# Attention turns in written groups: one TensorE order from the q columns to the output projection

## The chip, the cores and the metric

One core of a Trainium2 chip runs the kernel. The metric is device time in microseconds (us), the median of several runs; a profiled run, taken by itself, gives the trace. The engines are TensorE (PE, with its weight loads as PEld), VectorE (DVE), ScalarE (ACT), GpSimd (POOL) and SyncE (SP, which issues most DMAs).

## The reference, cut to what matters

The model is two layers over 256 tokens of width 2048, in float32. Layer one is an RWKV mixer, which this change leaves alone. Layer two is an attention with three branches that share keys and values by group; the change lies in it.

```python
proj = u @ w_in                                   # 16 heads of q, 48 gate columns, z
q = rope_partial(proj[..., :2048].reshape(B, T, 16, 128), arange(T))
gates = sigmoid(proj[..., 2048:2096] + gate_b)
# per head, with the keys of its group (4 heads to a group):
o_cmp = softmax(q @ k_cmp.T * scale, visible) @ v_cmp      # 15 compressed blocks
o_sel = softmax(q @ k_sel.T * scale, causal) @ v_sel       # all 4 blocks are selected
o_win = softmax(q @ k_win.T * scale, causal) @ v_win       # window 512 > 256 tokens
o = gates[0] * o_cmp + gates[1] * o_sel + gates[2] * o_win
h = h + (o * silu(z)) @ w_o
```

## The kernel before, in words

All large products are done in float32 precision as three products of a high and a low part (`whi`, `wlo` of a weight, `mx` or `ob` pairs of an activation): high by high, high by low, low by high. The weights come as raw pieces by SP's DMAs; for each unit ACT copies the high part (L213) and DVE subtracts to get the low one (L192; every third unit of the attention stage goes to POOL). Units are split three ahead of their use.

The stages are: normalisation and the columns of the RWKV mixer, its scan, its output projection with the residual, the kv columns with the compression (`phase_kv`), the attention stage, and the last output projection (`phase_bo`).

The attention stage has 21 dense phases, in the order of QZ (L81): five blocks of q columns (`phase_q`, 432, 512 and three times 384 columns, 16 k steps of six matmuls) and sixteen z columns (`phase_z`, heads 15 down to 0, each 16 k steps of a 512- and a 256-column matmul). The attention of the heads, pairs of heads from 7 down to 0, goes on beside them in background tasks. `Sched` (L97) holds a counter `sch.t`: each dense step yields its estimated nanoseconds, and after each the background tasks whose time has come go one step further. So the counter decides where in the program an instruction stands. Before, the program's place is only a rank for the scheduler of the framework, which orders each engine's queue by readiness in its own timeline and by rank; attention instructions on TensorE rank 1,000 places ahead (`atPE` in PRI, L93). The hardware then runs each engine's queue in order.

For one pair of heads the work is:

- q: a block is copied out of PSUM with its row scale (L1775), rotated on DVE (`rope`, L1628 to L1633), and turned on TensorE (transposed, two 128 x 128 pieces to a head, L1789) into a PT bank; ACT copies the high part, DVE subtracts the low one (L1792, L1793).
- scores (`weigh`, per head): nine matmuls (three parts, over 800 columns in all) into `pair0`, the only score tile, two PSUM banks wide; DVE adds masks and takes maxima (L1841 to L1846), ACT exponentiates with sums (L1853 to L1857), DVE takes reciprocals with the gates and scales the probabilities P0, P1 and Pcc (L1861 to L1866).
- turns (`turned`, per pair): P is transposed on TensorE in three sets of four (T0, T1, T2) and Pcc in one of two (T3), each into one of two PT banks; ACT copies the high part Th (L1888), DVE subtracts Tl (L1890, L1892).
- products: V's high and low parts by Th and Tl into the PV bank, twice three of 512 columns, twice three of 256, two of 256 for the compressed branch; ACT copies them out as og (L1921).
- `flush`: POOL multiplies by the gate z (L1935), ACT and POOL split the result (L1937, L1938) into the `ob` tiles, which the output projection reads, k from 15 down.

PSUM has eight banks: three for dense accumulators, two for turns (PT), one for products (PV), two for the scores. Each wait is a semaphore that the framework places. In the profile, instructions of `weigh` and `attend` on TensorE have line L244, that of the helper which ranks them; they are told apart by their tiles: `pair<-` scores, `bank<-cst,P` and `bank<-cst,pcc` turns, `bank<-Th` and `bank<-Tl` products. Lines L588 to L591 are q blocks and the output projection, L613 to L616 are z.

RST (L1754 to L1760) is the row scale of all tokens, turned so that it lies along the free dimension; z is multiplied by it (L1802).

## Time and profile before

| | |
|---|---|
| median of 3 runs | 1131.27 us (1128.8, 1131.27, 1133.68) |
| the profiled run | 1135.73 us, its span 1133.7 us |
| TensorE clock granted, mean | 0.996 |
| attention stage, first q matmul to the end of the first output block | 260.8 us |

The trace is one execution. The page gives shares of the span, the chain that ended last, and groups of instructions by line. Matmuls are pipelined: a record shows a matmul from its start to the end of its results, and the next one starts earlier than that, so a price per matmul is the distance from start to start. A releaser in brackets is what ended an idle time.

### The profile page before, as it was taken

The page shows a single profiled execution, that of the slowest core. Times are in us where ns is not written, and L with a number is a line of the kernel's source. Part 1 is how long each engine was busy: PE and PEld are TensorE (multiplying, and loading weights), DVE is VectorE, ACT ScalarE, POOL GpSimd, SP SyncE. Part 2 cuts the span into 40 slices and gives each one's busy share as a digit, 9 for nine tenths or more (in the row PEclk, how much of TensorE's full clock was granted, in tenths as well). Part 3 has the DMA queues.
Part 4 walks back from the last instruction along what each step waited for, and adds up shares of the span by engine and source line. Part 5 has one row for each costly group of instructions (what it writes and reads, how often), then busy time and mean ns, then how long its engine had stood idle before and what let it go on. Part 6 is the DMA issues. An engine that isn't in the chain of part 4 may idle for free.

```text
span 1133.7 us, 24534 instructions
## 1 busy us (share of the span) xinstructions
PE 1101.0 (97%) x8880; PEld 935.3 (83%) x8880; DVE 860.5 (76%) x1783; ACT 713.5 (63%) x1700; POOL 378.0 (33%) x487
## 2 busy tenths in 40 slices
PE   7999999999999999999999999999999999999997
PEld 7778899987788777877788888787889988888786
DVE  6998976789869797677567776764576888988564
ACT  5667688867665356655556766664666666666553
POOL 1400057755384546661010010101334435362212
PEclk9999999999999999999999999999999999999999
DMA  6568888976999968865457658585645453848562
GB/s 221 172 194 221 246 220 245 258 204 210 263 293 273 229 159 244 201 186 156 133 177 250 205 167 290 164 282 167 188 146 159 124 140 102 210 120 276 160 190 104
DMA packets 239033, 225.35 MB, mean 199 GB/s; under 512 B 58053, under 2 KB 185333, under 8 KB 238912
## 3 DMA queue, kind: packets, MB, share of 16 engines
q1 hardware_dynamic: 233472, 216.65, 65.8%
q0 software_dynamic: 5440, 7.14, 2.3%
q8 instruction: 70, 1.15, 0.5%
q14 instruction: 51, 0.42, 0.1%
HBM read 200.48 MB, written 23.10 MB: 197 GB/s over the span
## 4 chain that ended last, share of the span: by engine, by line
PE 73%; DVE 13%; DMA 4%; issue 4%; ACT 3%; POOL 2%; SPq 0%; ACTq 0%; POOLq 0%; DVEq 0%
PE bank L589 11%; PE bank L591 11%; PE bank L588 11%; PE bank L1348 5%; DVE wlo L192 5%; PE bank L613 4%; PE bank L614 2%; PE bank L607 2%; PE bank L1351 2%; PE bank L244 2%; PE bank L608 2%; PE bank L609 2%; PE pair L1370 2%; ACT whi L213 1%; PE pair L1372 1%
## 5 line engine op out<-in xcount | busy, mean ns | idle before, releaser
L192 DVE TENSOR_TENSOR wlo<-wraw,whi 128x512 fp32r<-128x512 f32 (+2 forms) x616 | 444.3, 738 | 164.1 <-ACT whi L213 161.6
L213 ACT ACTIVATE whi<-wraw 128x512 fp32r<-128x512 f32 (+2 forms) x661 | 397.9, 619 | 221.4 <-PE bank L591 79.7
L589 PE MATMUL bank<-wlo,mx 128*128 128x512 f32 (+3 forms) x576 | 216.1, 377 | 3.6 <-DVE wlo L192 2.7
L591 PE MATMUL bank<-whi,mx 128*128 128x512 f32 (+3 forms) x576 | 214.2, 374 | 0.0
L588 PE MATMUL bank<-whi,mx 128*128 128x512 f32 (+3 forms) x576 | 186.9, 376 | 1.8 <-ACT mx L428 0.9
L589 PEld LDWEIGHTS bank<-wlo,mx 128*128 128x128 f32 x576 | 108.3, 188 | 22.7 <-DVE wlo L192 5.4
L588 PEld LDWEIGHTS bank<-whi,mx 128*128 128x128 f32 x576 | 107.6, 188 | 19.1 <-ACT mx L1937 1.2
L591 PEld LDWEIGHTS bank<-whi,mx 128*128 128x128 f32 x576 | 108.3, 188 | 16.3 <-POOL mx L1938 0.4
L1348 PE MATMUL bank<-mx,whi 128*128 128x512 f32 x256 | 102.1, 430 | 0.0
L192 POOL TENSOR_TENSOR wlo<-wraw,whi 128x512 fp32r<-128x512 f32 (+2 forms) x48 | 63.1, 1316 | 110.6 <-ACT whi L213 88.7
L613 PE MATMUL bank<-mx,whi 128*128 128x512 f32 x240 | 86.8, 398 | 0.0
L607 PE MATMUL bank<-mx,whi 128*128 128x256 f32 (+1 forms) x288 | 83.0, 288 | 0.3 <-ACT mx L428 0.3
L608 PE MATMUL bank<-mx,whi 128*128 128x256 f32 (+1 forms) x288 | 81.4, 283 | 0.0
L609 PE MATMUL bank<-mx,wlo 128*128 128x256 f32 (+1 forms) x288 | 81.3, 282 | 0.0
L589 PE MATMUL bank<-wlo,kvh 128*128 128x512 f32 x192 | 76.9, 401 | 0.0
L591 PE MATMUL bank<-whi,kvl 128*128 128x512 f32 x192 | 76.1, 396 | 0.0
L614 PE MATMUL bank<-mx,wlo 128*128 128x256 f32 x256 | 70.6, 285 | 0.2 <-DVE wlo L192 0.2
L1351 PE MATMUL bank<-mx,wlo 128*128 128x256 f32 x256 | 70.5, 283 | 0.0
L588 PE MATMUL bank<-whi,kvh 128*128 128x512 f32 x192 | 67.4, 395 | 0.0
L1348 PEld LDWEIGHTS bank<-mx,whi 128*128 128x128 f32 x256 | 47.9, 189 | 10.5
L607 PEld LDWEIGHTS bank<-mx,whi 128*128 128x128 f32 (+1 forms) x288 | 54.2, 188 | 1.3 <-ACT mx L428 0.7
L609 PEld LDWEIGHTS bank<-mx,wlo 128*128 128x128 f32 (+1 forms) x288 | 54.2, 188 | 0.8 <-DVE wlo L192 0.2
(365 smaller groups left out, 2303.9 us busy)
## 6 DMA issues: line engine op xcount, KB each, us to landing
wraw<-in_a_w_rkvz_dram SPq DMA_DIRECT2D x128, 512.0 KB, 5.5
wraw<-in_kv_w_dram SPq DMA_DIRECT2D x48, 512.0 KB, 4.5
wraw<-in_b_w_in_dram SPq DMA_DIRECT2D x40, 512.0 KB, 4.2
wraw<-in_a_w_o_dram SPq DMA_DIRECT2D x32, 512.0 KB, 4.6
wraw<-in_b_w_o_dram SPq DMA_DIRECT2D x32, 512.0 KB, 4.3
spd<-sp SPq DMA_DIRECT2D x16, 642.0 KB, 4.4
wraw<-in_b_w_in_dram SPq DMA_DIRECT2D x24, 384.0 KB, 3.4
spl<-spd SPq DMA_DIRECT2D x14, 642.0 KB, 7.4
```

What stands on the lines that cost most here:

```text
L192: eng.tensor_tensor(lv, src, hv.bitcast(F32), op=OP.subtract)
L213: self.nc.scalar.activation(hv, src, AF.Copy, **self.mark)
L588: PE.matmul(o, mh[:, ts], wh[:, 0, :], start=k == ends[0], stop=False)
L589: PE.matmul(o, mh[:, ts], wl[:, 0, :], start=False, stop=False)
L591: PE.matmul(o, ml[:, ts], wh[:, 0, :], start=False, stop=k == ends[1])
L607: PE.matmul(o, wh[:, s, :], mh, start=k == 0 and first, stop=False, **kw)
L608: PE.matmul(o, wh[:, s, :], ml, start=False, stop=False, **kw)
L609: PE.matmul(o, wl[:, s, :], mh, start=False, stop=k == NK - 1, **kw)
L613: PE.matmul(o, wh[:, s, :], joint[nm, k], start=k == 0, stop=False, **kw)
L614: PE.matmul(o[:, :T], wl[:, s, :], mh, start=False, stop=False, **kw)
L1348: both = lambda: PE.matmul(o, wh[:, s, :], joint["r", k], start=k == 0, stop=k == NK - 1)
L1351: PE.matmul(o[:, :T], wl[:, s, :], mixed["r", k][0], start=False, stop=False)
```

## The change

It puts the TensorE instructions from the first q block to the end of the first output block into the order in which the program lists them (`tc.manual_schedule` for TensorE alone; the other engines are still ordered by the scheduler). The places in that order come from the counter, by four new constants:

- the turns of q become a background task, `turn_q`, that starts QTG after the block's evacuation, takes two heads (four pieces, 512 columns of one PT bank) at a time, and lists q as available 5,000 later;
- `weigh_all` is a task of its own and runs ahead of `attend`, limited by four buffers of P; WG stands between two heads;
- `attend` starts PG after the pair's last scores were weighed. T0 and T1 follow each other, then TG, then T2 and T3 and the products of T0 and T1, then TG, then the products of T2 and T3;
- the counter keeps a time from which each PT bank is free (`pt_free`, `pt_bank`).

P and the turned parts get four buffers instead of three (PB, TB). The block of q for heads 0 to 2 comes one z phase earlier in QZ. RST is made at the start of the kv stage, in the pool `bp`, and not at the start of the attention stage. The scratch for GpSimd's DMA descriptors is set to 8192. The numbers computed are the same.

```diff
+QTG, WG, PG, TG = 5000.0, 2400.0, 9000.0, 5500.0
-QZ = (0, 25, 24, 1, 2, 23, 22, 21, 3, 20, 19, 18, 4, 17, 16, 15, 14, 13, 12, 11, 10)
+QZ = (0, 25, 24, 1, 2, 23, 22, 21, 3, 20, 19, 4, 18, 17, 16, 15, 14, 13, 12, 11, 10)
-QTB, QB, PB, TB, OGB, RPB = 1, 8, 3, 3, 1, 1
+QTB, QB, PB, TB, OGB, RPB = 1, 8, 4, 4, 1, 1
...
+    RST = bp.tile([128, T], F32, name="RST")
...
+    def turn_rs():
+        pr = accp("tp")
+        for tt in range(2):
+            rb = bp.tile([128, 128], F32, name="rb", bufs=1)
+            V.tensor_copy(rb, RS[tt].to_broadcast([128, 128]))
+            PE.transpose(pr[:, tt * 128:(tt + 1) * 128], rb, ident)
+        V.tensor_copy(RST, pr[:, :T])
...
     cmpx = {}
+    turn_rs()
...
-    RST = at.tile([128, T], F32, name="RST")
-    pr = accp("PT")
...
     yield from rows_block(ps, "u", nc_)
+    sch.require(lambda: not turning)
...
-        sch.require(lambda: HEADS - h0 - used_q[0] <= QB)
-        for g in range(nh)[::-1]:
-            pt = accp("PT")[:, :T]
...
+        turning.append(n)
+        sch.add(turn_q(t, h0, nh))
+
+    PTS = dict(n=0, free=[0.0, 0.0])
+
+    def pt_free(n=1):
+        return all(PTS["free"][(PTS["n"] + i) % 2] <= sch.t for i in range(n))
+
+    def pt_bank(hold):
+        PTS["free"][PTS["n"] % 2] = sch.t + hold
+        PTS["n"] += 1
+        return accp("PT")
+
+    def turn_q(t, h0, nh):
+        yield QTG
+        yield lambda: HEADS - h0 - used_q[0] <= QB
+        for first in range(nh)[::-2]:
+            yield pt_free
+            heads = [first, first - 1][:first + 1]
+            both = pt_bank(3000.0)
+            for i, g in enumerate(heads):
+                for tt in range(2):
+                    PE.transpose(both[:, i * T + tt * 128:i * T + tt * 128 + 128], t[:, tt, g, :], ident)
+            for i, g in enumerate(heads):
...
+                S.activation(qh, pt, AF.Copy)
+                V.tensor_tensor(ql, pt, qh.bitcast(F32), op=OP.subtract)
+                sch.t += 215
+                qn.append((h0 + g, (qh, ql)))
+            yield 5000.0
+            qd.update(qn)
+            qn.clear()
+        turning.clear()
...
+    def weigh_all():
+        for p in range(HEADS // 2)[::-1]:
+            if p // 2 not in kvd:
+                split_kv(p // 2)
+            for h in (2 * p, 2 * p + 1):
+                yield lambda: len(weighed) < PB + 2 * len(turned_p)
+                P = yield from weigh(h)
+                weighed[h] = (P, sch.t)
+                yield WG
+
     def attend(p):
...
-        for h in (2 * p, 2 * p + 1):
-            P.append((yield from weigh(h)))
+        yield lambda: 2 * p + 1 in weighed and sch.t >= weighed[2 * p + 1][1] + PG
+        P = [weighed[h][0] for h in (2 * p, 2 * p + 1)]
...
+        yield lambda: pt_free(2)
         T0 = turned([w for P0, P1, _ in P for w in (P0[:, 0], P1[:, 0, 0:128])])
-        yield 500.0
         T1 = turned([w for P0, P1, _ in P for w in (P0[:, 1], P1[:, 1, 0:128])])
-        yield 500.0
+        yield TG
+        yield lambda: pt_free(2)
...
+        T2 = turned([P1[:, x, 128:256] for x in range(2) for _, P1, _ in P])
+        T3 = turned([Pcc for _, _, Pcc in P], True)[1].rearrange("p (i t) -> p i t", i=2)
+        turned_p.append(p)
         products(o, (vh[:, 0, 0], vl[:, 0, 0]), T0, start=True)
-        T2 = turned([P1[:, x, 128:256] for x in range(2) for _, P1, _ in P])
-        yield 500.0
         products(o, (vh[:, 1, 0], vl[:, 1, 0]), T1)
-        T3 = turned([Pcc for _, _, Pcc in P], True)[1].rearrange("p (i t) -> p i t", i=2)
-        yield 500.0
+        sch.t += 1400
+        yield TG
...
-        sch.t += 2600
+        sch.t += 1200
...
+    sch.add(weigh_all())
     sch.add(attn_all())
+    written = ExitStack()
+    written.enter_context(tc.manual_schedule(engines={PE.engine}))
...
         sch.require(lambda: not sch.bg)
+        written.close()
...
-    nc = _bacc.Bacc("TRN2", target_bir_lowering=False, num_devices=1)
+    nc = _bacc.Bacc("TRN2", target_bir_lowering=False, num_devices=1, dynamic_dma_scratch_size=8192)
```

## The prediction

> **What bounds the kernel now.** I read the page first, then the stretches of the attention stage, then TensorE's own timeline in it, then the chain.

> ```profile
> PE 1101.0 (97%) x8880; PEld 935.3 (83%) x8880; DVE 860.5 (76%) x1783; ACT 713.5 (63%) x1700; POOL 378.0 (33%) x487
> PE 73%; DVE 13%; DMA 4%; issue 4%; ACT 3%; POOL 2%; SPq 0%; ACTq 0%; POOLq 0%; DVEq 0%
> ```

> TensorE (PE) is busy 97% of the span and carries 73% of the chain. An edit that only reorders its work can win its waits and whatever the order itself costs, and no more. The change touches the stage from the first matmul of the q columns to the end of the first block of the output projection, which the timeline puts at 797.72 to 1058.49 us:

> ```profile
> core 0: us, PE busy (x) PEld busy (x) DVE busy (x) ACT busy (x) POOL busy (x), PEclk, DMA share, GB/s
> 797.72:1058.49 260.77, 257.95 (x1490) 230.83 (x1491) 207.21 (x422) 167.50 (x465) 103.05 (x96) 1.00 0.57 161
> 873.70:915.40 41.70, 40.34 (x246) 36.09 (x245) 37.29 (x74) 26.94 (x81) 17.77 (x16) 1.00 0.44 123
> 865.70:969.30 103.60, 101.36 (x620) 93.37 (x619) 89.53 (x188) 68.22 (x216) 42.38 (x40) 1.00 0.51 135
> ```

> Only 2.8 us of 260.77 are recorded as idle, at full clock. VectorE (DVE) is the engine to watch: 207.21 us over the stage, but 37.29 of 41.70 us (89.4%) in the second row, a stretch that the chain crosses on DVE, with short pieces on ScalarE (ACT) and of issue. I take 89% as what DVE can reach with this mix.

> The waits of TensorE are in its timeline. A record there is longer than its slot, so I read start to start:

> ```profile
> 906.59 0.33 PE L588 MATMUL bank<-whi,mx 128*128 128x384 f32 x1
> 906.76 0.34 PE L589 MATMUL bank<-wlo,mx 128*128 128x384 f32 x1
> 907.70 0.44 PE L1789 MATMUL bank<-cst,qt 128*128 128x128 f32 x2 [0.59 <-DVE ql L1793]
> ...
> 913.54 0.44 PE L589 MATMUL bank<-wlo,mx 128*128 128x384 f32 x1
> 914.09 0.33 PE L244 MATMUL bank<-cst,P 128*128 128x128 f32 x1
> ...
> 914.43 0.34 PE L589 MATMUL bank<-wlo,mx 128*128 128x384 f32 x1
> 915.40 0.66 PE L244 MATMUL bank<-cst,P 128*128 128x128 f32 x4 [0.63 <-DVE ql L1793]
> ...
> 960.09 0.59 PE L588 MATMUL bank<-whi,mx 128*128 128x384 f32 x2
> 961.56 0.45 PE L589 MATMUL bank<-wlo,mx 128*128 128x384 f32 x1 [0.88 <-POOL wlo L192]
> ...
> 971.96 0.40 PE L613 MATMUL bank<-mx,whi 128*128 128x512 f32 x1
> 972.54 0.39 PE L614 MATMUL bank<-mx,wlo 128*128 128x256 f32 x1 [0.19 <-DVE wlo L192]
> ...
> 1054.36 0.40 PE L591 MATMUL bank<-whi,mx 128*128 128x512 f32 x1
> 1055.16 0.50 PE L588 MATMUL bank<-whi,mx 128*128 128x512 f32 x1 [0.40 <-ACT mx L1937]
> ```

> A 384-column matmul takes 0.17 us of stream (906.59 to 906.76), a 512-column one 0.23 (below). What each gap has above that: 0.94 - 0.17 = 0.77; 0.55 - 0.17 = 0.38; 0.97 - 0.17 = 0.80; 1.47 - 0.34 = 1.13; 0.58 - 0.23 = 0.35; 0.80 - 0.23 = 0.57. Together 4.0 us. The first three end in a turn (a transpose): it needs a PT bank that DVE still reads, or P that DVE still scales. The next two wait for the low part of a weight. The last is the last heads' output.

> **The change, part by part.** The written order: from the first q column block to the first output block, TensorE takes its work as the program lists it, by the code's own counter, instead of as the scheduler ranks it (attention 1,000 ahead). The instructions are the same.

> *Turns in groups.* Counted in PE's timeline of the stage, the 144 turns (96 of P, 32 of q, 16 of Pc) stand in 68 runs, 32 of them single; written, they come as eight (T0 and T1), six (T2 and T3) and two or four (q), in 26 runs. What does a run cost?

> ```profile
> 937.57 0.28 PE L614 MATMUL bank<-mx,wlo 128*128 128x256 f32 x1
> 937.69 0.27 PE L244 MATMUL bank<-cst,P 128*128 128x128 f32 x1
> 937.72 0.48 PE L613 MATMUL bank<-mx,whi 128*128 128x512 f32 x1
> 938.03 0.28 PE L614 MATMUL bank<-mx,wlo 128*128 128x256 f32 x1
> 938.15 0.40 PE L613 MATMUL bank<-mx,whi 128*128 128x512 f32 x1
> 938.38 0.28 PE L614 MATMUL bank<-mx,wlo 128*128 128x256 f32 x1
> ```

> ```profile
> 849.40 0.60 PE L244 MATMUL bank<-cst,P 128*128 128x128 f32 x4
> 849.75 0.48 PE L589 MATMUL bank<-wlo,mx 128*128 128x512 f32 x1
> 850.07 0.40 PE L591 MATMUL bank<-whi,mx 128*128 128x512 f32 x1
> ```

> A plain 512-column matmul takes 0.23 us (938.15 to 938.38). The single turn costs 0.03, and the matmul behind it 0.31 instead of 0.23: 0.11 in all. The four cost 0.35, and the matmul behind them 0.32: 0.44, again 0.11 each. So a run has no fixed price that a longer run would spread: 144 x 0.11 = 15.8 us before and after, and the grouping itself is worth 0, between -0.5 and +0.5 us by the 10 ns to which the rows are read, over 42 runs.

> The group rows give another number, the mean duration:

> ```profile
> L244 PE MATMUL bank<-cst,P 128*128 128x128 f32 x96 | 17.5, 274 | 0.7 <-DVE ql L1793 0.6
> L1789 PE MATMUL bank<-cst,qt 128*128 128x128 f32 x32 | 5.2, 274 | 0.6 <-DVE ql L1793 0.6
> ```

> [...]

> *Parts read later.* Between a set of turns and the products that read them the counter now puts TG = 5,500 ns, between the pair's last weigh step and its turns PG = 9,000, between the q block and its turns QTG = 5,000. A counter nanosecond is a little more than one here: a k step of z counts 327 and takes 350 (938.03 to 938.38), three 384-column matmuls count 480 and take 520. The evacuation of a PT bank is one ACT copy and one DVE subtraction, so 5 us cover it even behind a queue. I let the first three waits go: -1.95 us. If that cover is gone, they stay.

> *The low parts.* DVE's work doesn't shrink, and the order packs it. The third window row runs from the scores of head 12 to those of head 5. Followed through its counter, the written order has those nine gaps at 8.8 to 10.8 us of count (7,900 from the yields of weigh and WG, plus what two turn sets, 430 each, or products, 1,400 or 1,200, add), which at 1.07 to 1.09 is 9.5 to 11.6, about 10.6 on average: 96 us for 103.6. About 88 us of DVE work lie there (89.53 less half a z step): 92%, over the 89.4% above, so DVE would need 98.4 us, 2.4 to 2.6 of waits. Against it: DVE idles on ACT within that share,

> ```profile
> 911.76 0.19 DVE L1861 RECIPROCAL rc<-sm 128x6 f32<-128x6 f32 x1 [1.36 <-ACT P L1857]
> ```

> and a fourth buffer for P and for the turned parts gives it other work to take there. I take half, 1.3 us (bounds 0 and 2.6), in place of the 1.13 now: +0.2. The wait at 971.96 (0.35) I let go, since less is due there.

> *RST moved.* Before, two copies and turns stand between the last kv matmul and the first q one:

> ```profile
> 796.72 0.40 PE L591 MATMUL bank<-whi,kvl 128*128 128x512 f32 x1
> 797.63 0.33 PE L1759 MATMUL bank<-cst,rb 128*128 128x128 f32 x1 [0.52 <-DVE rb L1758]
> 797.72 0.44 PE L588 MATMUL bank<-whi,mx 128*128 128x432 f32 x1
> ```

> TensorE waits 0.91 - 0.23 = 0.68 us, since rb lies in a pool that opens when the last kv matmul has read its tiles. In the kv stage the scheduler still orders PE and has dense work to put there: -0.68, and the two turns cost their 0.22 at either place. Without that cover the wait only moves: 0.

> *The end.* The last pair's products now have two k steps of the output block (2.7 us) behind them before their ob tiles are read, where the rows above show none in hand. I take 0.2 us for 0.57: -0.37.

> *q of heads 0 to 2 one z step earlier, smaller scratch.* The first only moves work within the order: 0. The scratch holds descriptors of GpSimd's DMAs; before, PE waits for those in one place:

> ```profile
> L1062 PE MATMUL pair<-Yb,a 64*64 64x32 f32 x256 | 7.5, 222 | 4.1 <-DMA Yb<-yvd 4.1
> ```

> No row shows a full queue, so 0, up to +4.1 if these waits doubled, below nothing excluded as less room speeds up no transfer.

> **Sum.** -1.95 + 0.2 - 0.35 - 0.68 - 0.37 = -3.15 us on the profiled run, which took 1135.73 us (span 1133.7). Its ratio is 0.9972; on the median, 1131.27, it gives 1128.1 us. The profiled run lies 4.5 us above the median, more than the whole effect: about 0.5%, 5.7 us, is what a measurement of this kernel can tell from no change.

> **Rivals.** *All waits go.* DVE fills every gap: -4.0 - 0.68 = -4.7, and small waits beside them 1 us more: 1125.6 to 1126.6, at the edge of what can be told. For it: slack of 5 us and more at every read. Against it: 92% of DVE.

> *The scores tile holds the order up (slower).* All heads share one pair of score banks; the next head's scores must wait until ACT has read the last:

> ```profile
> 887.56 0.29 PE L244 MATMUL pair<-kh,qh 128*128 128x272 f32 x1
> 899.22 0.24 ACT L1857 ACTIVATION_READ_ACCUMULATOR P<-pair,mx 128x1 f32 x1
> 900.99 0.29 PE L244 MATMUL pair<-kh,qh 128*128 128x272 f32 x1
> 911.50 0.23 ACT L1857 ACTIVATION_READ_ACCUMULATOR P<-pair,mx 128x1 f32 x1
> 911.85 0.33 PE L244 MATMUL pair<-kh,qh 128*128 128x272 f32 x1
> ```

> Scores to free tile took 11.9 and 10.7 us here; the written gaps average 10.6. It decides where this chain is longer than the gap, because behind the waiting scores stand all dense matmuls, in fixed order. At 11.9, nine gaps lose 9 x 1.3 = 11.7 us; less 4.7 gained, 1138. Against it: a waiting TensorE asks DVE for no weights, so DVE catches up.

> *A single turn costs its duration.* Then 42 runs fewer save 42 x (0.274 - 0.11) = 6.9 us more: 1121. The two timelines of runs speak against it.

> *The order comes out as before.* The scheduler's list may have had the same waits from DVE: 1131.

> **How the numbers follow.** My forecast has 0.44, all waits gone 0.20, the scores tile 0.18, the dear single turn 0.07, no change 0.11. Faster by over 0.5% (below 1125.6): 0.07, a bit over half of all waits gone, and 0.04 of the forecast's lower tail, 0.22. Slower (above 1136.9): 0.18 and 0.02 for the scratch, 0.20. The rest is 0.58. The range runs from 1122, which takes in all waits gone with the spread of the three runs shown (1128.8 to 1133.68) and leaves out half of the dear turn, to 1138, the scores tile at its price.

> **What would show it.** Right: turns in runs of 6 and 8 at 0.11 us each; no PE wait for ql, P or Th; PE idle in the stage near 1.5 us, what is left of it ended by wlo; first q matmul 0.23 us behind the last kv one; DVE at 90% or more between the scores of heads 12 and 5. Wrong: PE waits in front of the score matmuls (pair<-kh,qh) that ACT's L1857 ends (the scores tile); the stage at 250 us or less (turns cheaper in groups); a longer kv stage (RST not covered); longer waits for Yb.

## The result, and the profile after

The changed kernel takes 1143.04 us (median of 6 runs, 1141.78 to 1151.61) beside 1131.66 us for the kernel before on the same chip (6 runs). The ratio is 1.0109, 95% interval [1.0082, 1.0136]: slower, and above the range of the prediction. The profiled execution took 1151.61 us (span 1149.5) and is the slowest of the six. Of the 15.8 us between the two spans, 5.2 lie ahead of the first q matmul (802.93 us here, 797.72 before), in code that the change leaves as it was but for RST; the start of q moved between 791.7 and 802.9 us over the kernels profiled below. Between 20 us and the first q matmul TensorE was granted half its clock for 17.1 us here (around 241, 374 and 453 us), for 3.4 us in the profile before, and never in the kernel that starts q at 791.7: a loss of 6.8 us of full clock more, which is enough for these 5.2. So I compare one stretch, here called the stage: from the first q matmul to the first 256-column matmul of the output projection, which takes in whatever is late at the end.

The window views of that stretch, before and after, and four stretches inside it:

```profile
797.72:1102.01 304.29, 301.47 (x1682) 266.86 (x1683) 233.24 (x458) 190.59 (x506) 108.96 (x100) 1.00 0.58 165
```

```profile
core 0: us, PE busy (x) PEld busy (x) DVE busy (x) ACT busy (x) POOL busy (x), PEclk, DMA share, GB/s
802.93:1117.66 314.73, 304.38 (x1681) 271.00 (x1682) 236.89 (x455) 190.51 (x506) 110.74 (x101) 0.99 0.56 160
871.54:975.80 104.26, 97.83 (x597) 90.44 (x597) 87.95 (x189) 69.33 (x217) 43.68 (x40) 1.00 0.47 127
...
972.00:993.00 21.00, 15.09 (x76) 13.11 (x75) 17.43 (x35) 10.98 (x31) 6.80 (x6) 0.84 0.49 123
975.35:978.76 3.41, 3.34 (x13) 3.24 (x14) 3.41 (x10) 0.23 (x1) 1.36 (x1) 0.50 0.62 154
989.00:992.42 3.42, 3.42 (x13) 2.94 (x12) 1.63 (x4) 1.23 (x2) 0.00 (x0) 0.50 0.62 152
```

The stage is 10.44 us longer. TensorE's recorded idle went from 2.8 to 10.35 us (314.73 - 304.38). From 972 to 993 us the granted clock is 0.84, since it is 0.50 in the two stretches of 3.41 us of the last two rows. DVE is no busier than it was: 87.95 of 104.26 us, 84%, from the scores of head 12 to those of head 5, which in the kernel before was 89.53 of 103.60, 86%.

What TensorE waited for in the stage (total us, times, longest), after:

```profile
PE bank L245 <- DVE ql L1821: 3.9, 1, 3.9
PE bank L615 <- DVE wlo L193: 2.0, 1, 2.0
PE pair L245 <- ACT P L1890: 1.8, 2, 1.0
PE bank L614 <- ACT whi L214: 1.1, 1, 1.1
PE bank L615 <- POOL wlo L193: 1.0, 1, 1.0
PE bank L590 <- DVE wlo L193: 0.6, 1, 0.6
PE bank L589 <- ACT Vt L1702: 0.3, 1, 0.3
```

Start to start, as in the prediction, the six groups above the last are 4.13, 2.17, 1.14 and 1.00 (the two for the scores tile), 1.24, 1.28 and 0.76 us above the price of the matmuls: 11.7 us, where before had 4.0. The other 3 us or so stand behind the two longest. TensorE's timeline around them:

```profile
972.92 0.28 PE L615 MATMUL bank<-mx,wlo 128*128 128x256 f32 x1
973.03 0.39 PE L614 MATMUL bank<-mx,whi 128*128 128x512 f32 x1
975.42 0.58 PE L615 MATMUL bank<-mx,wlo 128*128 128x256 f32 x1 [2.00 <-DVE wlo L193]
...
977.84 0.63 PE L614 MATMUL bank<-mx,whi 128*128 128x512 f32 x1
978.27 0.41 PE L615 MATMUL bank<-mx,wlo 128*128 128x256 f32 x1
978.48 0.53 PE L614 MATMUL bank<-mx,whi 128*128 128x512 f32 x1
978.85 0.28 PE L615 MATMUL bank<-mx,wlo 128*128 128x256 f32 x1
978.97 0.40 PE L614 MATMUL bank<-mx,whi 128*128 128x512 f32 x1
...
984.00 0.60 PE L245 MATMUL bank<-cst,P 128*128 128x128 f32 x4
988.51 0.63 PE L245 MATMUL bank<-cst,P 128*128 128x128 f32 x4 [3.91 <-DVE ql L1821]
988.89 0.68 PE L614 MATMUL bank<-mx,whi 128*128 128x512 f32 x1
...
990.22 0.63 PE L614 MATMUL bank<-mx,whi 128*128 128x512 f32 x1
990.65 0.42 PE L615 MATMUL bank<-mx,wlo 128*128 128x256 f32 x1
```

Ahead of the wait a 256-column matmul takes 0.11 us (972.92 to 973.03); behind it a 512-column one takes 0.43 (977.84 to 978.27, 990.22 to 990.65) and a 256-column one 0.21, beside 0.23 and 0.11 at full clock, until 978.85, from where they take 0.12 again. Behind the second wait the same lasts until 992.5. Summed over the matmuls in these stretches, that is 1.5 and 1.8 us more, and two stretches of 3.41 us at half clock give 1.7 each: 7.7 us more of waits and 3.3 of half clock make 11.0 for the 10.44 measured.

Why the longest wait? T0 and T1 of the pair stand at 984.00, and T1 needs the PT bank into which q of two heads was turned at 980.74. ACT and DVE empty it so:

```profile
981.53 0.37 ACT L1820 ACTIVATE qh<-bank 128x256 fp32r<-128x256 f32 x1
982.33 0.37 ACT L1886 ACTIVATE P<-pair,mx 128x128 f32<-128x128 f32 x1 [0.44 <-DVE mx L1879]
...
985.25 0.41 ACT L1820 ACTIVATE qh<-bank 128x256 fp32r<-128x256 f32 x1
```

```profile
982.98 0.41 DVE L1821 TENSOR_TENSOR ql<-bank,qh 128x256 fp32r<-128x256 f32 x1
...
986.72 1.31 DVE L1899 TENSOR_TENSOR pcc<-Pc,rc 128x90 f32<-128x90 f32 x1
987.95 0.41 DVE L1821 TENSOR_TENSOR ql<-bank,qh 128x256 fp32r<-128x256 f32 x1
```

```profile
986.21 1.70 POOL L193 TENSOR_TENSOR wlo<-wraw,whi 128x512 fp32r<-128x512 f32 x1
```

The second head's qh stands behind the exponentials of another head on ACT (981.53, then 985.25), its ql behind that head's scaling on DVE (987.95). The bank is read for 7.6 us (980.74 to 988.36); the counter held it for 3,000 ns. Part of the delay on DVE lies beside POOL's work: the scaling of pcc takes 1.31 us here, beside POOL's subtraction of 1.70, and 0.24 at its shortest. In the stage, all 50 operations of DVE that took over one and a half times the shortest of their kind ran beside one of POOL, 37 us more than the shortest in all; before, it was 47 and 35 us. So this is no cost of the change, but it is one reason why a bank is held longer than one copy and one subtraction take.

### The profile page after: what moved, and what is told of

The parts are those of the page before. It is cut to its first block, busy times and chain, and to the rows that moved or that the text cites. A ratio compares the mean times of both kernels' runs of the same rounds, so it can differ in the third digit from the quotient of the medians.

```text
span 1149.5 us, 24532 instructions
## 1 busy us (share of the span) xinstructions
PE 1109.2 (96%) x8880; PEld 944.7 (82%) x8880; DVE 862.6 (75%) x1783; ACT 713.1 (62%) x1700; POOL 377.6 (33%) x487
## 5 line engine op out<-in xcount | busy, mean ns | idle before, releaser
L592 PE MATMUL bank<-whi,mx 128*128 128x512 f32 (+3 forms) x576 | 214.4, 374 | 0.0
L589 PE MATMUL bank<-whi,mx 128*128 128x512 f32 (+3 forms) x576 | 192.4, 376 | 1.8 <-ACT mx L429 1.0
L589 PEld LDWEIGHTS bank<-whi,mx 128*128 128x128 f32 x576 | 107.9, 188 | 18.8 <-ACT mx L429 1.2
L1349 PE MATMUL bank<-mx,whi 128*128 128x512 f32 x256 | 104.2, 438 | 0.0
L614 PE MATMUL bank<-mx,whi 128*128 128x512 f32 x240 | 89.2, 408 | 1.1 <-ACT whi L214 1.1
L589 PE MATMUL bank<-whi,kvh 128*128 128x512 f32 x192 | 68.0, 396 | 0.0
L1349 PEld LDWEIGHTS bank<-mx,whi 128*128 128x128 f32 x256 | 49.0, 193 | 10.8
```

The costliest lines, as they stand in the source:

```text
L589: PE.matmul(o, mh[:, ts], wh[:, 0, :], start=k == ends[0], stop=False)
L592: PE.matmul(o, ml[:, ts], wh[:, 0, :], start=False, stop=k == ends[1])
L614: PE.matmul(o, wh[:, s, :], joint[nm, k], start=k == 0, stop=False, **kw)
L1349: both = lambda: PE.matmul(o, wh[:, s, :], joint["r", k], start=k == 0, stop=k == NK - 1)
```

## The experiments

My theory: with holds and slacks shorter than what ACT and DVE take, the written order turns each late bank or late weight part into a stop of all of TensorE, and behind a long stop its clock can be halved besides, as behind those of 2.17 and 4.13 us above. The rivals: the regrouped turns or the shared bank cost by themselves; DVE is overloaded; the order is sound and RST, scratch or buffers cost. "Stage" is the stretch defined above: 304.29 us before, 314.73 after.

### Without the written order

```diff
-    written.enter_context(tc.manual_schedule(engines={PE.engine}))
```

> The changed kernel without the written order: the places that the counter gives are ranks for the scheduler again, all else stays (background turns, four buffers, RST in the kv stage). If the fixed order of the dense matmuls is the cause (they can't be passed over when a low part or a bank is late), nearly all of the loss goes: 0.997 to 1.001 of the kernel before. If the places themselves are bad (two heads to a PT bank, heads too close), the scheduler can only fill around them: 1.004 to 1.008.

1135.14 us, ratio 1.0041 [1.0022, 1.0060], stage 307.15. All other parts of the change, their new places included, are there; the turns stand in 45 runs and no wait is over 1 us. So some 7.6 of the 10.4 us come with the fixed order, and 2.9 with the places, of which no row here singles out one. Neither expectation holds alone: most of the loss goes, but what stays is above the first range and at the lower edge of the second.

### One head of q to a bank, written and ranked

```diff
-        for first in range(nh)[::-2]:
+        for first in range(nh)[::-1]:
-            heads = [first, first - 1][:first + 1]
+            heads = [first]
-            yield 5000.0
+            yield 2500.0
```

> The changed kernel, but the turns of q take one head to a PT bank (as before the change) with half the pause behind it, still in the written order. If the bank that two heads share is the main cause, the wait of 4.1 us for ql in front of T1 of pair 3 goes, and with it the 3 us or so of matmuls at half clock behind it: 1.0109 becomes about 1.005. If late low parts and the scores tile are the cause, under 2 us change: 1.009 to 1.011.

1141.04 us, 1.0105 [1.0068, 1.0142], stage 311.78. The waits moved more than they shrank: 3.40 us for ql with half clock behind it and 1.19 for another ql, 2.01 for wlo, 1.51 and 1.03 for Tl. The same edit without the written order:

> The changed kernel without the written order and with one head of q to a PT bank. If the shared bank is what still costs 0.4% in the version without the written order (its waits of 0.5 to 0.9 us end mostly in turns), this comes to 0.999 to 1.002. If the late reading or the order of the tasks is, it stays at 1.003 to 1.005.

1139.98 us, 1.0078 [1.0048, 1.0109], stage 308.95; my expectation, level with before, failed. The two heads in one bank are not what costs most: with one head to a bank the ranked kernel's stage comes out no shorter (307.15 with two), and the written one's loses 2.95 us, with waits of 3.40 and 2.01 left.

### Longer hold for the q bank

```diff
-            both = pt_bank(3000.0)
+            both = pt_bank(8000.0)
```

> The changed kernel with the counter keeping a PT bank of q taken for 8,000 instead of 3,000. If a bank that is read for longer than the counter thinks is the main cause, the wait in front of T1 goes as in the run with one head to a bank: about 1.005. If low parts and the scores tile are, 1.009 to 1.011, or a little worse, since pair 3 comes later and the rest is packed closer.

1137.72 us, 1.0059 [1.0038, 1.0080], stage 307.81. This one number takes the wait for ql away and 6.9 us off the stage. What is left: 1.28 and 0.93 for weights, and the last pair is now late by 2.17 us at the end, with half clock behind it (512 columns take 0.43 us).

### More room between the scores of two heads

```diff
-QTG, WG, PG, TG = 5000.0, 2400.0, 9000.0, 5500.0
+QTG, WG, PG, TG = 5000.0, 3600.0, 9000.0, 5500.0
```

> The changed kernel with 3,600 instead of 2,400 of count between two heads (WG). If heads that follow too closely are the main cause (the scores tile, and DVE and ACT packed between), the two waits for ACT in front of scores (2.1 us) and about half of the 6 us of waits for low and high parts go: about 1.005, and the attention ends later. If the shared bank is, nothing goes or it only moves: 1.009 to 1.012.

1140.51 us, 1.0093 [1.0072, 1.0115], stage 311.02: in time the same as the change, by these intervals. The waits for the scores tile went, and others came with the shifted places: a q turn 3.59 us behind a P set's low part, the end 2.17, both with half clock (256 columns take 0.16 us behind the first, 512 columns 0.43 behind the second).

### The parts beside the order

RST and scratch alone, on the kernel before:

```diff
+    turn_rs()
...
-    RST = at.tile([128, T], F32, name="RST")
...
+    nc = _bacc.Bacc("TRN2", target_bir_lowering=False, num_devices=1, dynamic_dma_scratch_size=8192)
```

> The kernel before, with RST made in the kv stage and the scratch at 8192 (which makes the room), nothing else. If both are harmless, as forecast: the first q matmul comes 0.2 to 0.7 us earlier behind the last kv one and the time is 0.998 to 1.001. If one of them costs the 2 to 4 us by which the written versions lie above what their attention stage explains, 1.002 to 1.004, with a longer scan or kv stage.

1132.36 us, 1.0013 [0.9997, 1.0029], stage 304.25. Its first q matmul in TensorE's timeline:

```profile
793.74 0.40 PE L591 MATMUL bank<-whi,kvl 128*128 128x512 f32 x1
794.44 0.47 PE L588 MATMUL bank<-whi,mx 128*128 128x432 f32 x1 [0.31 <-ACT Vt L1701]
```

The wait for rb is gone and one for ACT's copy Vt stands behind it: 0.70 us for the 0.91 of before. With four buffers besides:

```diff
-QTB, QB, PB, TB, OGB, RPB = 1, 8, 3, 3, 1, 1
+QTB, QB, PB, TB, OGB, RPB = 1, 8, 4, 4, 1, 1
```

> The kernel before, with three parts of the change and none of the written order: four buffers instead of three for the probabilities and for the turned parts, RST made in the kv stage, the smaller scratch. Theory (the written order alone costs): the two extra buffers give the scheduler more freedom and nothing else, so 0.997 to 1.002 of before and a stage of 303 to 305 us (304.29 before; RST and scratch alone gave 304.25). Rival (the buffers let work on DVE and ACT run ahead of the low parts, and so cost by themselves): new waits for wlo over 1 us, stage above 306 us, 1.004 or more.

1135.27 us, 1.0021 [1.0003, 1.0040], stage 303.60, with the waits of before. In the stage these parts cost nothing; whether they cost 1 or 2 us outside it, these intervals do not settle.

### Less work for DVE in the changed kernel

```diff
-APOOL = 3
+APOOL = 2
```

> The changed kernel, with every second low part of the stage on POOL instead of every third. It tells whether DVE's load is what the written order runs into. Rival (DVE's load, as the prediction had it): the waits that DVE's wlo ends, 2.17 and 0.76 us, go, and with the first its half clock, 1.6 us; 1.011 becomes 1.006 to 1.008, and the 4.13 us wait for ql shrinks, as DVE reaches it earlier. Theory (the holds are too short for the chain ACT, DVE, ACT, whatever DVE's load): the wait for ql stays over 3 us, waits that POOL's wlo ends grow from 1.24 to 2 us or more, since POOL's subtraction is the slower one, and the time stays at 1.009 to 1.015.

1144.15 us, 1.0109 [1.0086, 1.0132], stage 313.12. DVE has 230.17 us in the stage instead of 236.89, POOL 138.84 instead of 110.74, and TensorE's three longest waits are for what they were for:

```profile
PE bank L245 <- DVE ql L1821: 4.4, 1, 4.4
PE bank L590 <- DVE wlo L193: 1.8, 1, 1.8
PE pair L245 <- ACT P L1890: 1.7, 2, 0.9
```

With 3% less for DVE, the signs of the rival did not come: the wait for ql is 4.57 us start to start and one for DVE's wlo 1.96. My theory missed too, in the waits for POOL's wlo, which shrank from 1.0 to 0.4 in the view. So this run gives no support to DVE's load as the cause, nor to the way in which my prediction had costed the low parts. It does not rule out a larger relief, since POOL's 28 us more stand beside DVE's operations, which are stretched there (42 us more than their shortest in all, for 37).

### Longer holds, and places for them

```diff
-QTG, WG, PG, TG = 5000.0, 2400.0, 9000.0, 5500.0
+QTG, WG, PG, TG = 5000.0, 2400.0, 6000.0, 4500.0
-QZ = (0, 25, 24, 1, 2, 23, 22, 21, 3, 20, 19, 4, 18, 17, 16, 15, 14, 13, 12, 11, 10)
+QZ = (0, 25, 24, 1, 2, 23, 22, 21, 3, 20, 4, 19, 18, 17, 16, 15, 14, 13, 12, 11, 10)
-            both = pt_bank(3000.0)
+            both = pt_bank(8000.0)
-            pt = pt_bank(3500.0)[:, :n]
+            pt = pt_bank(5500.0)[:, :n]
```

> The changed kernel in written order, with a counter that keeps the PT banks as long as the trace shows them read (8,000 for q, 5,500 for P), and that makes up for it at the end (PG 6,000, TG 4,500, q of heads 0 to 2 one z block earlier still), so that the last pair's products keep 7 us in hand. If banks that the counter frees too early are the main cause, no wait over 2 us and no half clock are left, and it is 1.000 to 1.004. If a fixed order of the dense matmuls costs by itself (late low parts), 1.005 or more, with waits for wlo and whi.

1136.47 us, 1.0038 [1.0015, 1.0061], stage 305.13: still in the written order, 9.6 us of the 10.44 are back. No wait reaches 2 us and no half clock follows (1.00 granted over the stage). The waits that are left are for weights in the main (1.7, 1.0 and 0.7 us in the view of waits). The hold of q alone gave 6.9 us; which of the other edits gave the rest, this run does not tell.

### Weights split further ahead

Four ahead instead of three, in the ranked kernel with RST and scratch, throughout and then in the stage alone (there with the change's QZ); both have six weight buffers instead of five.

```diff
-RAWB, AHEAD, SPLB = 5, 3, 2
+RAWB, AHEAD, SPLB = 5, 4, 2
```

> The kernel before, with RST in the kv stage, scratch 8192 and weights split four units ahead instead of three (the room that the change gave to P and the turned parts goes to the weights). If late low parts are a cost of their own in this stage, the waits for wlo (1.5 us) go: 0.995 to 0.999. If DVE is simply full there, nothing: 0.999 to 1.002.

1135.35 us, 1.0035 [1.0017, 1.0053], above both expectations, though the stage is short: 302.91. Every wait for wlo is gone; the end waits 2.17 us for the last pair, with half clock behind it (512 columns take 0.43 us). The scan begins at 358.73 us instead of some 354.

```diff
+    W.ahead = 4
...
-        pool, bufs = (self.pool, self.ahead + 2) if self.split < self.kept_from else (self.kept_pool, 8)
+        pool, bufs = (self.pool, 6) if self.split < self.kept_from else (self.kept_pool, 8)
```

> Ranked order, not written: the kernel before with RST in the kv stage, the smaller scratch, the changed place of the q block of heads 0 to 2, and units of weights split four ahead instead of three in the attention stage alone (six buffers). With four ahead everywhere the stage took 302.91 us with a wait of 2.17 us at its end, and what came before it was longer. Theory (TensorE waits mostly for low parts; the last pair is then what is late): no wait for wlo over 0.3 us, and if the earlier q block brings the last pair forward, no wait over 1 us at the end: stage 301 to 302.5 us, 0.995 to 0.999. If the last pair ends no earlier, the end's wait stays near 2 us with its half clock, stage 303 us, 0.998 to 1.001.

1133.81 us, 1.0021 [1.0005, 1.0037], stage 302.25: the stage as expected, the time not; the end still waits 1.18 us. The same two lines in the written order with the longer holds:

> The written order with the longer holds and slacks of the run before it (q bank 8,000, P bank 5,500, PG 6,000, TG 4,500), three buffers for the turned parts, and weights split four ahead in the attention stage. That run had 305.13 us for the stage, with waits of 1.87 (wlo), 1.28 (whi), 1.09 (qt), 0.87 (wlo) and 0.75 us (Tl). Theory (what is left over in the written order are late weights and a few turns): the waits for whi and wlo go, 3.5 to 4 us in all, stage 301 to 303 us, level with the best ranked version, 0.996 to 1.000. Rival (a fixed order turns any slack given to weights into lateness of the turns, as ACT and DVE do the weights first): turns' waits of 1 us and more in their place, stage 304 to 307 us, 1.002 to 1.006.

1129.92 us, 0.9983 [0.9969, 0.9997], stage 300.36. All its waits over 0.2 us in the stage:

```profile
PE bank L1816 <- DVE qt L1644: 0.7, 1, 0.7
PE pair L245 <- ACT P L1891: 0.5, 1, 0.5
```

Now the stage in written order is 1.9 us shorter than in the ranked kernel with six buffers (302.25), which lacks the change's background turns and its fourth buffer of P, and 3.9 shorter than before. Is it the place of the split or the sixth buffer? Four ahead out of five buffers, with long holds and with the changed kernel's own:

```diff
+    W.ahead = 4
...
-        pool, bufs = (self.pool, self.ahead + 2) if self.split < self.kept_from else (self.kept_pool, 8)
+        pool, bufs = (self.pool, AHEAD + 2) if self.split < self.kept_from else (self.kept_pool, 8)
```

> Written order, long holds and slacks (q bank 8,000, P bank 5,500, PG 6,000, TG 4,500), weights split four ahead in the attention stage, but with the five weight buffers of the kernel before: with six, the stage was 300.36 us (304.29 before), while the scan began at 359.39 us instead of 353.59 in the same kernel with five. Theory (the six buffers cost some 5 us ahead of the scan; the stage's gain comes from the earlier splits): scan start at 354 to 356 us, stage 300 to 302 us, 0.993 to 0.997 of before. Rival one (five buffers give no room to split four ahead, as each split waits for the unit just read): the waits of 0.9 to 1.9 us for wlo come back, stage 303 to 305.5 us, 0.998 to 1.004. Rival two (the later scan has another cause): scan start at 359 us, 0.997 to 0.999.

> The changed kernel as it stands (holds 3,000 and 3,500), with weights split four ahead in the attention stage out of the same five buffers. With the changed kernel, the one with long holds, and that with both it makes a table of two by two. Theory (the holds and the late weights cost by themselves, and the short q hold the most): the waits for wlo and whi of 2.17, 1.28, 1.24 and 0.76 us shrink or go, the one for ql of 4.13 us with its 1.6 us of half clock stays or grows, stage 308 to 312 us, 1.005 to 1.009. Rival (the late weights are only what a turn that comes too early pushes back, so only the holds matter): stage 313 to 316 us as in the changed kernel, 1.010 to 1.014. Rival two (the turns wait only because DVE is behind with low parts): the wait for ql goes too, stage below 306 us, 1.003 or less.

With long holds 1137.30 us, 1.0056 [1.0034, 1.0078], stage 305.06; with short ones 1143.32 us, 1.0123 [1.0086, 1.0159], stage 313.72. Both theories failed, and by the stage the first rival of each fits: four ahead is nothing without the buffer. The last kernel has the sixth buffer in the stage alone:

```diff
...
+        if self.extra is not None and self.split % 6 == 5:
+            pool, bufs, sfx = self.extra, 1, "x"
...
+    W.ahead, W.extra = 4, at
```

> Written order with long holds and slacks, weights split four ahead in the attention stage, three buffers for the turned parts, and a sixth weight buffer that exists in the attention stage only (every sixth unit goes to a buffer of the stage's own pool). With six buffers throughout, the stage was 300.36 us and the scan began at 359.39 us; with five, 305.06 and 353.95. Theory (the sixth buffer gives the stage its gain, and its cost ahead of the scan comes from being there then): scan start 353 to 355 us, stage 300 to 302.5 us, 0.994 to 0.998 of before. Rival (what made the stage shorter was not the buffer): stage 304 to 306 us, 1.003 to 1.006. Second rival (the buffer does it, but the later scan start was chance): stage 300 to 302 us, scan start near 359 us, 0.997 to 1.000.

1129.42 us, 0.9986 [0.9967, 1.0004], stage 300.29, scan start 354.10. Together, the stage in us:

| written order | 3 ahead, 5 buffers | 4 ahead, 5 buffers | 4 ahead, 6 buffers |
|---|---|---|---|
| holds 3,000 and 3,500 | 314.73 (the change) | 313.72 | |
| holds 8,000 and 5,500, PG, TG and QZ with them | 305.13 | 305.06 | 300.36, 300.29 |

With four ahead, the sixth buffer is what makes the stage shorter, and the later scan start comes with having it from the beginning. Two things were not run: six buffers with three ahead, and the sixth buffer with the short holds. The kernels of the last column also have three buffers for the turned parts, those of the others four. But the medians don't carry the whole gain: a stage 4.0 us shorter than before gave 1.6 us less (from 3.7 less to 0.5 more, by the interval), and the two kernels at 305 us are 4 to 6 us above before by their ratios.

A part of this is clock in the executions that weren't profiled. The mean granted clock over all executions is 0.9926 and 0.9923 in the two kernels at 305 us, 0.9915 and 0.9936 in the two at 300, and 0.9944 to 0.9953 in the kernel before, each time on the same chip. Times the span of some 1130 us, that is 1.9 to 3.3 us of full clock less, an estimate of what it can cost at most. (In the changed kernel the mean is 0.9893.) Where in those executions the half clock lies, and the 2 us or so that are left in one of the kernels at 305 us, stays open.

## Why the prediction was wrong

**The first three waits (-1.95 us): the step that failed.** "The evacuation of a PT bank is one ACT copy and one DVE subtraction, so 5 us cover it even behind a queue." The rows quoted ahead of that sentence spoke against it: q is turned at 907.70 and the P turn at 915.40 waits for its ql, 7.7 us in one bank. I took from them the wait, 0.80, and not the 7.7, which is how long the bank was held. I also set 5 us against the time until parts are read, while the hold that decides when the bank is written again was 3,000. In the ranked order the scheduler put dense matmuls between, and 0.80 us of those 7.7 became a wait; in the written one the bank was read for 7.6 us against the 3,000 ns held, and the wait was 4.13. With 8,000 ns, one number, it is gone, and 6.9 us of the stage with it.

**The price of a stop.** The sum had none beyond its length, since no wait of before was over 1.13 us. Behind each of the two longest stops here the clock was halved for 3.41 us: 3.3 us of cost in this stage.

**The low parts (+0.2).** Late weights cost 5.4 us (2.17, 1.28 and 0.76 for low parts, 1.24 for a high one) instead of 1.3. I costed them as DVE's saturation, 92% asked and 89.4% to be had. DVE had 84%, and it stood idle for 1.70 us ahead of the late part, for ACT's exponentials, behind which the next high parts stood too (ACT copies them from 971.91 on):

```profile
969.70 0.68 DVE L193 TENSOR_TENSOR wlo<-wraw,whi 128x512 fp32r<-128x512 f32 x1
972.08 0.19 DVE L1894 RECIPROCAL rc<-sm 128x6 f32<-128x6 f32 x1 [1.70 <-ACT P L1890]
...
974.69 0.68 DVE L193 TENSOR_TENSOR wlo<-wraw,whi 128x512 fp32r<-128x512 f32 x1
```

```profile
971.91 1.18 ACT L214 ACTIVATE whi<-wraw 128x512 fp32r<-128x512 f32 x2
```

A chain over ACT and DVE was late by these rows, while DVE still had idle time: the low part of 974.69, behind the scaling of P, is what ends the wait of 2.17. 3% less work for DVE left a wait of 1.96 for it, while longer holds with a sixth buffer and splits four ahead took the waits for weights away. The wait at 971.96 that I let go has its like in the one of 2.17: both stop the z block behind the q block of heads 0 to 2, but at different weights (heads 7 and 8), since that block moved.

**RST (-0.68)** brought 0.21 (0.91 to 0.70, in the kernel with RST and scratch alone): behind rb stood another wait, Vt's. I named "the wait only moves" and gave it no weight.

**The end (-0.37)** held in the changed kernel, where no wait over 0.2 us is left there; but the last pair is next in line whenever the rest gets faster (1.18 to 2.17 us in four experiments).

**Grouping (0), scratch (0)** were right, the scratch as far as can be told: with RST and scratch alone TensorE waits 3.6 us for Yb, where before has 4.1 and the changed kernel 5.2. An eight in TensorE's timeline after:

```profile
861.36 0.34 PE L592 MATMUL bank<-whi,mx 128*128 128x384 f32 x1
861.54 1.03 PE L245 MATMUL bank<-cst,P 128*128 128x128 f32 x8
862.33 0.42 PE L589 MATMUL bank<-whi,mx 128*128 128x384 f32 x1
862.59 0.33 PE L590 MATMUL bank<-wlo,mx 128*128 128x384 f32 x1
```

0.79 for the eight and 0.26 instead of 0.17 behind them: 0.88, 0.11 each, as for one. The turns do stand in 26 runs.

**The rivals.** The scores tile stopped TensorE twice, for 2.14 us in all and not 11.7, and it decided little: with more room these waits went, others came, and the time stayed. "All waits go" was no property of this change, but of the written order with right holds and one more buffer: two waits, 0.7 and 0.5 us in the view, are left there. The slower side had 0.20 and its top, 1138, was one mechanism; that several late parts each stop a fixed order was missing.

## What to carry to other kernels

Before work is put into a fixed order, measure from the trace how long each shared buffer is really held, from the write to the last read, at its longest, and set the holds and spare buffers by that; here the scheduler hid all but 0.80 us of a bank held for 7.7 us, while the written order paid 4.13 for one held 7.6. Ask of every wait not only how long it was but how long the thing it waited for took. And when one number is mended, look for the next in line, since here the waits moved on (ql, then weights, then the last pair) until holds, places and buffers fitted together.

## What the runs showed of the hardware

By start to start, stops of 1.77, 1.87, 1.96 and 2.01 us left the clock full in four kernels (512 columns took 0.23 us behind the first two, 272 columns 0.12 or 0.13 behind the others); 2.02 us in another, 2.17 in four and those from 3.40 to 4.57 were each followed by half clock.

So in these runs the length alone does not part the two outcomes, as a pair shows. The stop of 2.02 us, in the kernel with short holds and four ahead, lies whole in the 3.41 us ahead of the half clock (first two rows: TensorE busy for 1.57 of 3.41 us, then clock 0.50). The one of 2.01 us, in the written order with one head of q to a bank, is spread over two stretches of 3.41 us (last two rows: busy for 2.36 and 2.63 us), and the clock stayed full:

```profile
965.75:969.16 3.41, 1.57 (x12) 1.34 (x11) 3.41 (x7) 2.39 (x5) 2.41 (x2) 1.00 0.29 76
969.16:972.58 3.42, 3.42 (x13) 2.94 (x12) 3.35 (x10) 0.63 (x1) 0.43 (x1) 0.50 0.59 153
```

```profile
962.89:966.30 3.41, 2.36 (x14) 2.04 (x12) 3.34 (x6) 3.13 (x7) 2.93 (x3) 1.00 0.01 2
966.30:969.71 3.41, 2.63 (x17) 2.59 (x18) 3.38 (x5) 0.92 (x2) 1.88 (x2) 1.00 0.48 112
```

What parts the two is not shown by one pair.
